# The order of a chunk's products in the recurrence of an RWKV-7 mixer: the keys' products ahead of the state's

## The chip, the core and the metric

The kernel runs on one core of one Trainium2 chip. The metric is the device time of one execution in microseconds, as the median of several runs. The profile is of one execution, and it shows each engine's instructions: TensorE (PE, with its weight loads as PEld), VectorE (DVE), ScalarE (ACT), GpSimd (POOL) and SyncE (SP), which issues the DMAs.

## What is computed

One decoder layer over 512 tokens of width 1024: a combined projection, a dilated attention, an RWKV-7 time mixing, gates, an output projection and a gated feed-forward part with a short convolution. The change lies in the time mixing, which for each of 16 heads (64 by 64 state) is this recurrence over the tokens:

```python
def step(state, inp):
    r_t, w_t, k_t, v_t, aa_t, bb_t = inp
    sa = jnp.einsum('bhvk,bhk->bhv', state, aa_t)
    state = state * w_t[:, :, None, :] + sa[..., None] * bb_t[:, :, None, :] + v_t[..., None] * k_t[:, :, None, :]
    return state, jnp.einsum('bhvk,bhk->bhv', state, r_t)
```

Each token's `sa` depends on the state, and so on the tokens before it.

## The kernel before

**Stages.** First come the attention's projections and scores, then, in one long stage written with a planner (`rwkv`, line 1041), the projections of the time mixing, the recurrence, the branch gates and the attention's output projection; then the mixer's output, and the feed-forward part with its up and down products. Float32 products of weights are made of three products of halves (high by high, high by low, low by high, lines 156 to 172), each with 512 moving columns.

**The recurrence.** It doesn't go token by token. 512 tokens are cut into 8 chunks of 64 (`NCH`, line 31). The 16 heads are 8 pairs, and a group g (0 to 3) holds two pairs, i = 0 and 1, four heads. `pair` (line 1223) prepares r, k, v and the scaled rows of a pair; its `ar` holds for each chunk the rows that are multiplied with the state, one half for what is solved for and one half for the outputs, and `gt` holds the masked products of these rows with the keys. `inverse` (line 1436) turns the triangular system of each chunk into a matrix, mostly on VectorE in many short steps (tiles `tt` and `lt`, lines 1500 to 1526). `chain` (line 1572) then goes through the 8 chunks c of a group, and these steps follow each other for each chunk:

- `values` and `value` (1591 to 1602): v of two chunks on TensorE into the PSUM tile `u`, then two copies on ScalarE into the tile `uv`. They are made once for two chunks, behind the update of an odd chunk, for the next two.
- `state` (1625): the right-hand side of what is solved for, in the PSUM tile `xy`: the state's share (two products, `ar` with the state `mbd`, 128 rows by 64 columns of the array, 128 moving columns; not for c = 0) and the keys' share (four products, `gt` with `uv`, 64 by 64, 64 moving columns).
- `state_out` (1633): the state's share of the outputs, two products like those of the state above, in the PSUM tile `xo`.
- `xs` (1639) copies `xy` on ScalarE, `solve` (1649) multiplies with the inverse, `solved` (1653) copies the result into `uv`.
- `update` (1656): four products for the new state into the other half of the tile `u`; `carry` (1661) makes the new state `mbd` of each pair from it on VectorE; `mp` (1643) has scaled the old one on GpSimd before.
- `outs` and `out` (1668 to 1675): the keys' share of the outputs, added in `xo`, and its copy.

**What sets the order.** `Plan` (line 47) holds tasks with an engine, an estimated time in microseconds, what they depend on, a priority (a smaller number goes first) and rooms in buffers that they take and give back. Its `run` (line 68) simulates the engines by these estimates, with 0.2 between engines, and emits each task's instructions when the simulation starts it. So it fixes the order on each engine; on the chip each engine works through that order and waits on semaphores. Tasks of the chain have priority 0 or a little over it (`C_`), the steps of evicting PSUM 1, weights 2 and more, the products of the projections 10 and more, the pairs' work and the inverse about 200. So a product of a projection goes where TensorE would have nothing of the chain to do: these are the fillers, and the rows of the timeline name their tiles (pg for the gates, pa for the attention's output, k, r and v for the projections of the pairs). A filler is booked at 0.237 (line 1119).

The lines that book the two tasks of the change, before it:

```python
st = pe(0.6 if c else 0.33, state, [uvd[c], start] + mb, take=("xy",), name=f"xy{g}.{c}")
so_ = pe(0.33 if c else 0.0, state_out, [st], C_ + 0.01, take=("xo",), name="xo")
x = sca(0.29, xs, [st], take=("xs",), give=("xy",))
```

`state` depends on the values (`uvd`) and on the carried state (`mb`) alike; in the plan it starts when both are there.

Of the kernel before, what the change touches and what calls it, by code (L numbers as in the profile page):

```python
# [18 lines left out]
P = 128  # L19
# [98 lines left out]
C_, E_, W_, V_, I_, M_, S_, U_ = 0.0, 1.0, 2.0, 200.0, 200.15, 220.0, 1.0, 10.0  # L118
# [10 lines left out]
class Layer:  # L129
# [1442 lines left out]
    def chain(self, g):  # L1572

        nc, pl, cw = self.nc, self.pl, self.cw
        prs, gr = self.prs[g], self.grp[g]
        ps = lambda s, **kw: self.cps.tile([P, 512], F32, tag=s, name=self.n(s), **kw)
        mbd = lambda i: self.mbd[2 * (g % 2) + i]
# [4 lines left out]
        pe = lambda us, fn, deps, prio=C_, **kw: pl.add("PE", us, fn, deps, prio, **kw)  # L1582
# [27 lines left out]
        def vals(c):  # L1610
            t = pe(0.54, lambda: values(c), [start, last_uv])
            t = sca(0.38, lambda: value(c, 0), [t], C_, take=("uv",))
            uvd[c] = uvd[c + 1] = sca(0.38, lambda: value(c, 1), [t], C_)
        vals(0)
        for c in range(NCH):
            e, q, cp = c % 2, c // 4, (c % 4) // 2

            R = [slice(64 * (e ^ i), 64 * (e ^ i) + 64) for i in range(2)]
            X = R[::-1]
            gt = lambda i, h, rows, cols, e=e, q=q, cp=cp: prs[i]["gt"][rows, e ^ i, 4 * q + 2 * cp + h, cols]  # L1620
            s = {}

            ih = [(i, h, slice(h * 64, h * 64 + 64), slice(i * P + h * 64, i * P + h * 64 + 64)) for h in range(2) for i in range(2)]

            def state(c=c, s=s, gt=gt, R=R, X=X, ih=ih):
                xy = s["xy"] = ps("xy")
                s["uv"] = uvs[c - c % 2][:, c % 2]
                for i in range(2 if c else 0):
                    self.mm(xy[X[i], :P], prs[i]["ar"][:, c, X[i]], mbd(i), True, False)
                for i, h, cs, ci in ih:  # L1630
                    self.mm(xy[X[i], cs], gt(i, h, R[i], X[i]), s["uv"][R[i], ci], c == 0 and h == 0, h == 1)

            def state_out(c=c, s=s, R=R):

                s["xo"] = ps("xo")
                for i in range(2 if c else 0):
                    self.mm(s["xo"][R[i], :P], prs[i]["ar"][:, c, R[i]], mbd(i), True, False)

            def xs(s=s):
                s["xs"] = cw.tile([P, P], F32, tag="xs", name=self.n("xs"), bufs=1)  # L1640
                nc.scalar.copy(s["xs"], s["xy"][:, :P])

            def mp(c=c, s=s):
                s["mp"] = cw.tile([P, 2, P], F32, tag="mp", name=self.n("mp"), bufs=1)
                for i in range(2):
                    nc.gpsimd.tensor_scalar(s["mp"][:, i, :], mbd(i), prs[i]["pc"][:, c : c + 1], 0.0, op0=ALU.mult,
                                            op1=ALU.add)

            def solve(s=s, gt=gt, X=X, ih=ih):
                for i, h, cs, _ in ih:  # L1650
                    self.mm(d["u"][X[i], cs], gt(i, h, X[i], X[i]), s["xs"][X[i], cs], h == 0, h == 1)

            def solved(i, s=s, X=X):
                nc.scalar.copy(s["uv"][X[i], i * P : i * P + P], d["u"][X[i], :P])

            def update(c=c, q=q, s=s):
                for j, (i, h, cs) in enumerate(hs):
                    self.mm(d["w"][64 * h : 64 * h + 64, cs], prs[i]["bkt"][q][:, c % 4, 64 * h : 64 * h + 64],
                            s["uv"][:, cs], j < 2, j > 1)

            def carry(i, c=c, s=s):
                ws, pc = d["w"][:, i * P : (i + 1) * P], prs[i]["pc"][:, c : c + 1]
                if c:
                    nc.vector.scalar_tensor_tensor(mbd(i), ws, pc, s["mp"][:, i, :], op0=ALU.mult, op1=ALU.add)
                else:
                    nc.vector.tensor_scalar(mbd(i), ws, pc, 0.0, op0=ALU.mult, op1=ALU.add)

            def outs(c=c, s=s, gt=gt, R=R, ih=ih):
                for i, h, cs, ci in ih:
                    self.mm(s["xo"][R[i], cs], gt(i, h, slice(0, P), R[i]), s["uv"][:, ci], c == 0 and h == 0, h == 1)  # L1670

            def out(c=c, s=s):
                if c % 2 == 0:
                    yts[c // 2] = cw.tile([P, 2, P], F32, tag=f"yt{c // 2}", name=self.n("yt"), bufs=1)
                nc.scalar.copy(yts[c // 2][:, c % 2, :], s["xo"][:, :P])

            st = pe(0.6 if c else 0.33, state, [uvd[c], start] + mb, take=("xy",), name=f"xy{g}.{c}")
            so_ = pe(0.33 if c else 0.0, state_out, [st], C_ + 0.01, take=("xo",), name="xo")
            x = sca(0.29, xs, [st], take=("xs",), give=("xy",))
            mpt = pl.add("POOL", 1.06, mp, mb, C_, take=("mp",)) if 0 < c < NCH - 1 else None  # L1680
            so = pe(0.33, solve, [x, last_uv], give=("xs",), name="u")
            last_uv = sca(0.28, lambda solved=solved: solved(0), [so])
            last_uv = sca(0.28, lambda solved=solved: solved(1), [last_uv])
            prev = mb
            if c < NCH - 1:
                up = pe(0.5, update, [last_uv], name="w")
                mb = [dve(0.36, lambda i=i, carry=carry: carry(i), [up, mpt, so_], give=("mp",) if mpt and i else ())
                      for i in range(2)]
            if e and c < NCH - 1:
                vals(c + 1)  # L1690
            ou = pe(0.35, outs, [last_uv, so_], C_ + 0.02, name="xr")
            yt = sca(0.29, out, [ou], C_ + 0.05, take=("yts",) if c == 0 else (), give=("xo",))
            used.extend([ou] + ([up] if c < NCH - 1 else []))
            if e:
                pl.join(used, give=("uv",))
                used = []
            d["yt", c] = yt
            if e:
                norms.append(self.norm(yts, c // 2, [yt, d["yt", c - 1]], T_))
# [474 lines left out]
```

## Time and profile before

| | us |
|---|---|
| median of 3 runs | 1232.48 |
| lowest, highest | 1231.15, 1234.05 |
| the profiled execution | 1231.16 |
| its span in the trace | 1229.4 |
| recurrence of g0, first to last xy product | 443.6 to about 488 |
| recurrence of g3, to its last xy product | from 708.5 to 750 |

The span is what the trace shows from the first to the last instruction; the rest of the execution's own time lies around it. The granted clock of TensorE is 0.982 of full speed over the span. In the page, busy times are given with their share of the span; a matmul's end is modelled, so that products which follow each other overlap in the rows, and the distance of two starts says what one costs. In a row of the timeline stand start, length, engine, line, operation, the tile written and the tiles read, the tile of the array (rows * columns) for a matmul, partitions by elements and type, and the count of records that were merged; in brackets the idle time of the engine before it and what ended it. Products of float32 are recorded as two passes each. All matmuls stand at line 148, the helper that issues them, so they are told apart by the tiles they write and read.

### The profile page before, as it was taken

Reading aid. Unit: us, or ns where it says so; the run is one execution under the profiler, and the core shown is the slowest. Engines: PE = TensorE matmul, PEld = TensorE weight load, DVE = VectorE, ACT = ScalarE, POOL = GpSimd, SP = SyncE. Lnnn points to the kernel's source line nnn. Section 1 sums busy time; section 2 is a strip of 40 time slices with the busy share of each in tenths; the row PEclk is TensorE's granted clock in tenths of the full one; section 3 lists DMA queues with packets and bytes.
Section 4 is the critical chain, followed back from the end, with each engine's and each line's share of the span. In section 5 each row is a group of like instructions: output and inputs, shape, how many; then the busy total and the mean of one; then the engine's idle time right before and its main releaser. Section 6 shows DMA issues by size and latency. Waiting matters only on the chain.

```text
span 1229.4 us, 18443 instructions
## 1 busy us (share of the span) xinstructions
PE 1179.8 (96%) x7188; PEld 946.3 (77%) x7188; DVE 746.0 (61%) x1254; ACT 542.6 (44%) x1009; POOL 120.3 (10%) x235
## 2 busy tenths in 40 slices
PE   4999999999999999999999599999999999999997
PEld 3788888889777876767776467788888888878886
DVE  6687862431678977846896844665556555652135
ACT  4384621522566364464544443444444444442123
POOL 4000000000001013131103122214000000000001
PEclk9899999999999999999999699999999999999999
DMA  9845871130233332413231525560232323333331
GB/s 317 248 142 157 284 236 46 52 86 5 81 100 84 98 108 72 127 44 116 78 99 49 159 60 177 154 206 18 69 103 86 103 86 103 86 103 103 103 120 69
DMA packets 168902, 139.41 MB, mean 113 GB/s; under 512 B 8849, under 2 KB 150251, under 8 KB 168815
## 3 DMA queue, kind: packets, MB, share of 16 engines
q1 hardware_dynamic: 168671, 137.98, 37.0%
q8 instruction: 56, 0.92, 0.3%
q14 instruction: 31, 0.25, 0.1%
q10 hardware_dynamic: 144, 0.26, 0.1%
HBM read 127.65 MB, written 10.56 MB: 112 GB/s over the span
## 4 chain that ended last, share of the span: by engine, by line
PE 82%; DVE 9%; DMA 4%; ACT 2%; issue 1%; SPq 0%; POOL 0%; POOLq 0%; DVEq 0%; ACTq 0%
PE u L148 22%; PE o L148 13%; PE v L148 7%; PE pg L148 7%; PE qk L148 6%; PE pr L148 3%; PE r L148 3%; PE k L148 3%; PE pa L148 3%; DMA araw<-in_w_ada_dram 2%; PE early L148 2%; PE po L148 2%; PE xy L148 2%; PE pt L151 1%; PE xo L148 1%
## 5 line engine op out<-in xcount | busy, mean ns | idle before, releaser
L194 DVE TENSOR_TENSOR wlo<-raw,whi 128x1024 fp32r<-128x1024 f32 x67 | 83.9, 1252 | 152.6 <-ACT whi L193 152.6
L148 PE MATMUL u<-h2lo,whi 128*128 128x512 f32 (+2 forms) x368 | 142.3, 387 | 0.0
L148 PE MATMUL u<-h2hi,whi 128*128 128x512 f32 (+2 forms) x368 | 142.2, 387 | 0.0
L148 PE MATMUL u<-h2hi,wlo 128*128 128x512 f32 (+2 forms) x368 | 142.2, 386 | 0.0
L1136 ACT CAST whi<-raw 128x1024 fp32r<-128x1024 f32 (+2 forms) x73 | 72.5, 994 | 122.7 <-PE qk L148 49.5
L193 ACT CAST whi<-raw 128x1024 fp32r<-128x1024 f32 x67 | 70.3, 1049 | 112.1 <-PE o L148 53.8
L1139 DVE TENSOR_TENSOR wlo<-raw,whi 128x1024 fp32r<-128x1024 f32 (+2 forms) x73 | 83.7, 1149 | 19.1 <-ACT whi L1136 18.8
L148 PEld LDWEIGHTS u<-h2lo,whi 128*128 128x128 f32 x368 | 68.9, 187 | 15.8 <-POOL h2lo L405 0.2
L148 PEld LDWEIGHTS u<-h2hi,wlo 128*128 128x128 f32 x368 | 68.9, 187 | 15.7
L148 PEld LDWEIGHTS u<-h2hi,whi 128*128 128x128 f32 x368 | 68.9, 187 | 15.4
L2019 DVE SCALAR_TENSOR_TENSOR u<-u,cols,u 128x511 f32<-128x511 f32 x88 | 65.7, 746 | 4.3 <-ACT u L2017 2.7
L148 PE MATMUL qk<-hhi,wlo 128*128 128x512 f32 x160 | 64.0, 400 | 0.0
L148 PE MATMUL qk<-hlo,whi 128*128 128x512 f32 x160 | 63.6, 397 | 0.0
L148 PE MATMUL qk<-hhi,whi 128*128 128x512 f32 x160 | 63.5, 397 | 0.0
L148 PE MATMUL o<-whi,fhi 128*128 128x512 f32 x144 | 56.1, 390 | 0.3 <-DVE u L2019 0.3
L148 PE MATMUL o<-whi,flo 128*128 128x512 f32 x144 | 56.0, 389 | 0.0
L148 PE MATMUL o<-wlo,fhi 128*128 128x512 f32 x144 | 56.0, 389 | 0.0
L148 PE MATMUL pg<-hhi,wlo 128*128 128x512 f32 x128 | 51.8, 405 | 0.0
L148 PE MATMUL pg<-hlo,whi 128*128 128x512 f32 x128 | 51.7, 404 | 0.0
L148 PE MATMUL pg<-hhi,whi 128*128 128x512 f32 x128 | 51.7, 404 | 0.0
L810 DVE CUSTOM_DVE_ANT_0 sm<-sc,m 128x256 f32<-128x256 f32 (+1 forms) x64 | 23.9, 404 | 37.6 <-PE sc L148 36.5
L347 DVE SCALAR_TENSOR_TENSOR acc<-araw,cols,acc 128x1024 f32<-128x1024 f32 x28 | 35.9, 1281 | 15.9 <-DMA araw<-in_w_ada_dram 15.8
(409 smaller groups left out, 2779.1 us busy)
## 6 DMA issues: line engine op xcount, KB each, us to landing
raw<-in_w_in_dram SPq DMA_DIRECT2D x62, 512.0 KB
raw<-in_w_up_dram SPq DMA_DIRECT2D x44, 512.0 KB
araw<-in_w_ada_dram SPq DMA_DIRECT2D x32, 512.0 KB
raw<-in_w_down_dram SPq DMA_DIRECT2D x22, 512.0 KB
araw<-in_w_ada_dram SPq DMA_DIRECT2D x32, 256.0 KB
wvraw<-in_w_in_dram SPq DMA_DIRECT2D x20, 256.0 KB
gate_d<-gs SPq DMA_DIRECT2D x16, 256.0 KB
gate<-gate_d SPq DMA_DIRECT2D x16, 256.0 KB
```

The source lines that it names most:

```text
L148: return self.nc.tensor.matmul(out, lhsT, rhs, start=start, stop=stop)
L151: self.nc.tensor.matmul(out, in_, self.ident[: in_.shape[0], : in_.shape[0]], is_transpose=True, start=start, stop=stop,)
L193: self.nc.scalar.copy(hl[0], raw)
L194: (lo_eng or self.nc.vector).tensor_tensor(hl[1], raw, hl[0], op=ALU.subtract)
L347: nc.vector.scalar_tensor_tensor(d["acc"], raw, ck, d["acc"], op0=ALU.mult, op1=ALU.add)
L810: nc.vector.tensor_tensor_reduce(d["sm", h][:, :wd], d["sc"][h][:, :wd], m[:, 256 - wd : 256] if gi == 0 else m[:, :wd], 1.0, 3.0e38, op0= ...
L1136: nc.scalar.copy(d["w"][0], d["raw"])
L1139: nc.vector.tensor_tensor(d["w"][1], d["raw"], d["w"][0], op=ALU.subtract)
L2019: nc.vector.scalar_tensor_tensor(u[:, d:], pu[:, : S - d], ch(c), u[:, d:], op0=ALU.mult, op1=ALU.add)
```

## The change

Within `state` the four products of the keys' share go first and open the accumulation in `xy`, and the two products of the state's share follow and close it. `state_out` is booked at 0.24 instead of 0.33, and its priority becomes -1 instead of 0.01, so that nothing else that is ready on TensorE goes between the two tasks. What is summed up is the same; only the order of the sums in `xy` differs.

```diff
             def state(c=c, s=s, gt=gt, R=R, X=X, ih=ih):
                 xy = s["xy"] = ps("xy")
                 s["uv"] = uvs[c - c % 2][:, c % 2]
+                for i, h, cs, ci in ih:
+                    self.mm(xy[X[i], cs], gt(i, h, R[i], X[i]), s["uv"][R[i], ci], h == 0, c == 0 and h == 1)
                 for i in range(2 if c else 0):
-                    self.mm(xy[X[i], :P], prs[i]["ar"][:, c, X[i]], mbd(i), True, False)
-                for i, h, cs, ci in ih:
-                    self.mm(xy[X[i], cs], gt(i, h, R[i], X[i]), s["uv"][R[i], ci], c == 0 and h == 0, h == 1)
+                    self.mm(xy[X[i], :P], prs[i]["ar"][:, c, X[i]], mbd(i), False, True)
...
             st = pe(0.6 if c else 0.33, state, [uvd[c], start] + mb, take=("xy",), name=f"xy{g}.{c}")
-            so_ = pe(0.33 if c else 0.0, state_out, [st], C_ + 0.01, take=("xo",), name="xo")
+            so_ = pe(0.24 if c else 0.0, state_out, [st], C_ - 1.0, take=("xo",), name="xo")
             x = sca(0.29, xs, [st], take=("xs",), give=("xy",))
```

## The prediction

> **What bounds the kernel now.** The page first, for the share of each engine and for the chain that ended last.
>
> ```profile
> span 1229.4 us, 18443 instructions
> PE 1179.8 (96%) x7188; PEld 946.3 (77%) x7188; DVE 746.0 (61%) x1254; ACT 542.6 (44%) x1009; POOL 120.3 (10%) x235
> PE 82%; DVE 9%; DMA 4%; ACT 2%; issue 1%; SPq 0%; POOL 0%; POOLq 0%; DVEq 0%; ACTq 0%
> ```
>
> TensorE is busy for 96% of the span and carries 82% of the last chain, so a microsecond taken from its queue can count in full. An average says nothing about one stage, so the busy times by window come next, cut at the recurrences of the four groups (g0 to g3). The columns are window, length, then PE, PEld, DVE, ACT and POOL busy time, granted clock, DMA share, GB/s.
>
> ```profile
> 440.00:490.00 50.00, 50.00 (x481) 34.96 (x480) 34.53 (x84) 27.15 (x70) 13.59 (x26) 1.00 0.29 84
> 515.00:560.00 45.00, 44.68 (x447) 30.73 (x447) 22.86 (x42) 25.79 (x66) 13.22 (x23) 1.00 0.27 77
> 640.00:690.00 50.00, 46.87 (x462) 32.18 (x460) 37.39 (x89) 23.19 (x64) 13.53 (x25) 0.94 0.26 82
> 690.00:706.00 16.00, 5.58 (x135) 4.68 (x137) 13.59 (x24) 8.67 (x15) 2.17 (x3) 0.50 0.59 166
> 706.00:755.00 49.00, 49.00 (x440) 32.63 (x439) 20.40 (x42) 21.09 (x61) 10.46 (x22) 0.94 0.25 74
> ```
>
> The recurrences of g0, g1 and g3 run with TensorE full (50.00 of 50, 44.68 of 45, 49.00 of 49): products of the projections fill what a chunk leaves free. Between g2 and g3 lies the one hole, 690 to 706: TensorE 5.58 of 16, VectorE 13.59 of 16. There VectorE decides. So there are two kinds of place: where TensorE is full, its own time for a chunk counts; in the hole, what lets VectorE finish the inverse of g3 sooner.
>
> **What the change saves on TensorE.** The timeline of TensorE over an odd chunk, c = 5 of g0, and the update after it. Here xy<-mbd is the state's share of what is solved for, xy<-uv the keys' share, xo<-mbd the state's share of the outputs; 4 or 8 records are the passes of 2 or 4 products.
>
> ```profile
> 474.11 0.40 PE L148 MATMUL pg<-hhi,wlo 128*128 128x512 f32 x1
> 474.44 0.44 PE L148 MATMUL xy<-mbd,ar 128*64 128x128 f32 x4
> 474.81 0.45 PE L148 MATMUL xy<-uv,gt 64*64 64x64 f32 x8
> 475.19 0.44 PE L148 MATMUL xo<-mbd,ar 128*64 128x128 f32 x4
> 475.56 0.50 PE L148 MATMUL pg<-hhi,whi 128*128 128x512 f32 x1
> ...
> 477.95 0.45 PE L148 MATMUL u<-uv,bkt 128*64 128x64 f32 x8
> 478.24 0.61 PE L148 MATMUL u<-cen,v 128*64 128x128 f32 x8
> 478.68 0.40 PE L148 MATMUL xo<-uv,gt 128*64 128x64 f32 x8
> ```
>
> Read the starts, since the ends are modelled. The three groups take 0.37, 0.38 and 0.37 us, and the array's tiling goes 128*128, 128*64, 64*64, 128*64, 128*128: four switches. The lower rows show the same kind of product between neighbours of its own tiling: u<-cen,v, eight records of 128x128 at 128*64, starts at 478.24 and is followed at 478.68, so eight take 0.44 and four take 0.22. Between two switches four take 0.37. The change puts the 64*64 group first, then both 128*64 groups behind each other: one switch fewer, and 0.37 - 0.22 = 0.15 us less.
>
> How often: the rows of the two groups, by tile.
>
> ```profile
> L148 PE MATMUL xy<-mbd,ar x112: 272/323/474, 449.1 to 749.5; 128*64 128x128 f32 x112
> L148 PE MATMUL xo<-mbd,ar x112: 272/323/473, 449.9 to 750.3; 128*64 128x128 f32 x112
> ```
>
> 112 records by 4 are 28 chunks: c = 1 to 7 of four groups (c = 0 has no state, and its products don't change). In the timeline of all 28 the xo group already stands right behind the xy group, so the new priority of the outputs' share moves nothing by itself. Saved at most: 28 x 0.15 = 4.2 us.
>
> **What it costs: the keys' values are the later arrival.** An even chunk, c = 6 of g0, in the timeline of all engines. VectorE's carry makes mbd, ScalarE's two copies (L1602) make uv.
>
> ```profile
> 478.96 0.61 DVE L1664 SCALAR_TENSOR_TENSOR mbd<-u,pc,mp 128x128 f32<-128x128 f32 x2 [1.78 <-PE u L148]
> ...
> 479.66 0.76 ACT L1602 COPY uv<-u 64x256 f32<-64x256 f32 x2 [2.41 <-DVE mbd L1664]
> ...
> 480.13 0.44 PE L148 MATMUL xy<-mbd,ar 128*64 128x128 f32 x4
> ...
> 480.50 0.45 PE L148 MATMUL xy<-uv,gt 64*64 64x64 f32 x8
> ```
>
> mbd is ready at 479.57 (478.96 + 0.61), uv at 480.42 (479.66 + 0.76), because both read the PSUM tile u and the copies wait for the carry. Today the state's products run from 480.13 to 480.50 and cover just this lateness. With the keys first nothing does: the queue stands from 480.13 until 480.42, about 0.30 with the start. The planner won't put the chunk later: it books the values as before. That TensorE waits for uv in just this way shows in c = 4 of g0, the first even chunk where uv is late; the last is c = 6 of g3.
>
> ```profile
> 468.37 0.53 PE L148 MATMUL xy<-mbd,ar 128*64 128x128 f32 x4
> 468.45 0.37 ACT L1602 COPY uv<-u 64x256 f32<-64x256 f32 x1 [0.49 <-DVE mbd L1664]
> ...
> 468.83 0.48 PE L148 MATMUL xy<-uv,gt 64*64 64x64 f32 x8
> ```
>
> ```profile
> 743.41 0.76 ACT L1602 COPY uv<-u 64x256 f32<-64x256 f32 x2 [2.43 <-DVE mbd L1664]
> ...
> 743.87 0.44 PE L148 MATMUL xy<-mbd,ar 128*64 128x128 f32 x4
> ```
>
> In the first, the copy ends at 468.82 and the keys start at 468.83; the new queue would stand from 468.37 to 468.83, 0.46. In the last, the copies end at 744.17 and the place in the queue is 743.87: 0.30. So it is in 9 of the 12 even chunks c = 2, 4, 6: two in g0, three in g1, one in g2, three in g3. Together 8 x 0.30 + 0.46 = 2.9 us of standing. Odd chunks take values copied a chunk earlier and don't wait.
>
> The Trainium skill (TensorE: Matmul & The Clock Gate, Part 2, on what happens when a matmul is issued) says that only weight loads are pulled ahead and that the matmuls stay in program order; this speaks against the change, and the row at 468.83 agrees. Were the products behind free to overtake a waiting one, nothing of the 2.9 would be lost.
>
> **Where the keys first do help.** Where mbd is the later arrival the keys fill the wait: c = 4 and c = 7 of g2.
>
> ```profile
> 667.27 0.92 PE L148 MATMUL xy<-mbd,ar 128*64 128x128 f32 x4
> ...
> 667.36 0.35 DVE L1664 SCALAR_TENSOR_TENSOR mbd<-u,pc,mp 128x128 f32<-128x128 f32 x1 [0.51 <-ACT uv L1602]
> ...
> 668.12 0.45 PE L148 MATMUL xy<-uv,gt 64*64 64x64 f32 x8
> ```
>
> ```profile
> 684.75 0.95 PE L148 MATMUL xy<-mbd,ar 128*64 128x128 f32 x4 [1.49 <-DVE mbd L1664]
> 685.63 0.69 PE L148 MATMUL xy<-uv,gt 64*64 64x64 f32 x8
> 686.25 0.69 PE L148 MATMUL xo<-mbd,ar 128*64 128x128 f32 x4
> ```
>
> At c = 4 the group takes 0.85 instead of 0.37 since the second carry is late; the keys (0.38) fit into that: 0.4 saved. At c = 7 the keys (0.62 at the lower clock) fit into the wait of 1.49; but the hole follows, so I count neither these 0.62 nor the 0.15 of that chunk.
>
> **The sum.** On TensorE: -27 x 0.15 + 2.9 - 0.4 = -1.55 us. By group: g0 -1.05 + 0.76 = -0.3; g1 -1.05 + 0.90 = -0.15; g2 (c = 1 to 6) -0.90 + 0.30 - 0.40 = -1.0; g3 -1.05 + 0.90 = -0.15. g3's share reaches the end, as only full TensorE follows at once. The rest has to pass the hole, which ends when VectorE is through.
>
> ```profile
> 659.98 0.61 DVE L1664 SCALAR_TENSOR_TENSOR mbd<-u,pc,mp 128x128 f32<-128x128 f32 x2 [2.87 <-PE u L148]
> ...
> 678.75 0.61 DVE L1664 SCALAR_TENSOR_TENSOR mbd<-u,pc,mp 128x128 f32<-128x128 f32 x2 [0.94 <-ACT uv L1602]
> 679.28 0.56 DVE L1512 TENSOR_TENSOR tt<-tt,lt 128x400 f32<-128x400 f32 x1
> ...
> 705.49 0.27 DVE L1589 MEMSET u<- 128x256 f32 x1
> ```
>
> VectorE works through its queue in order, and g3's inverse (tt, lt) stands behind the carries, which wait for the chunk: 2.87 us at 659.98, still 0.94 at 678.75. From there it hardly stands until the memset at 705.49 that starts g3. So what g2 saves up to its fifth chunk (-0.85) passes. Of g0 and g1 (-0.45) I count half: between them and g2 lies a stretch where VectorE is nearly full. That gives -0.15 - 0.85 - 0.2 = -1.2 us. Bounds of this case: -0.15 if only g3's share arrives, -1.55 if all does.
>
> **The planner's number.** 0.33 becomes 0.24, so the plan thinks each of 28 chunks 0.09 shorter, 2.5 us in all. Near the change it moves nothing: before the solve it still fits two filler products (0.6 + 0.24 + 2 x 0.237 = 1.31, against a copy ready at 0.6 + 0.2 + 0.29 + 0.2 = 1.29, by its own costs). Further off a step may change places; I take 0, and bound it by one to three such steps as the one of 0.56 at 679.28, either way: about 1.5 us.
>
> So the profiled execution (1231.16 us, span 1229.4) would become 1230.0. It lies 1.3 below the median of the runs, 1232.48; from that, -1.2 gives 1231.3 us. A measurement of this kernel can tell about 0.2%, 2.5 us, from no change: this is no measurable change.
>
> **Rivals.** *The values come in time.* If the plan's shift puts one more filler ahead of the even chunks, or ScalarE's copies go ahead of the carry, nothing stands: -27 x 0.15 - 0.4 = -4.45, 1228.0 us, faster. For it: in 3 of the 12 even chunks uv isn't late today. Against: 9 are late by nearly the same 0.30, and copies and carry follow each other. The Trainium skill (PSUM — Partial Sum Buffer, on bank collisions) holds that two engines must not touch one bank at once, reads included; the copy that starts at 479.66, 0.09 behind the carry's end, fits that, so only a change of their order would help.
>
> *The hole grows.* The plan thinks the chunks shorter while the even ones get 0.15 longer (0.30 - 0.15), so VectorE stands longer at g2's carries, with g3's inverse behind them. If at each of six carries one step of 0.56 goes from before the wait to behind it, the hole ends 6 x 0.56 = 3.4 us later: 1232.5 + 3.4 less g3's 0.15, 1235.7 us, slower. For it: the wait of 2.87 at 659.98 shows that such waits occur with nothing in front. Against: the carries at 678.75 and 684 hardly wait. It decides once the memset that starts g3 comes over 2.5 us later than at 705.49.
>
> *Joining saves nothing,* because the second pair of weights costs a start of its own: then 2.9 - 0.4 = +2.5 us is left, 1235.0, at the edge of slower. Against it stand the eight records in 0.44.
>
> **How the numbers follow.** Forecast 0.57, values in time 0.23, hole 0.15, no saving 0.05. Part of the forecast's case, with the 1.5 us of the plan in its favour, passes -2.5: I give that 0.03. Faster 0.23 + 0.03 = 0.26; slower 0.15 and half of the last, 0.17; same 0.57. The forecast's own range is 1231.3 with 1.5 of the plan and its bounds, 1229.4 to 1233.8. To leave out no more than 2 in 10 the range must reach both outer cases: 1228.0 to 1235.7.
>
> **What would show it.** Right: xy<-uv ahead of xy<-mbd and xo<-mbd in all 28 chunks; the two mbd groups together about 0.60 instead of 0.37 + 0.37; waits of PE xy for ACT uv L1602 of about 0.3 in most even chunks, nearly 3 us in sum; the memset of g3 about 1 us earlier; g3 from there to its last chunk unchanged within 0.3. Wrong: no such waits (the first rival), a hole that ends over 2.5 us later (the second), or 0.74 for the joined groups (the third).

## The result, and the profile after

The changed kernel takes 1242.82 us (median of 3 runs, 1242.26 to 1244.67) against 1232.48: ratio 1.0084, 95% interval 1.0062 to 1.0105. It is 10.3 us slower; the prediction had 1231.3 and a range up to 1235.7. The profiled execution took 1242.26 us. Its page:

```profile
span 1240.5 us, 18454 instructions
PE 1182.6 (95%) x7188; PEld 948.6 (76%) x7188; DVE 746.9 (60%) x1254; ACT 542.3 (44%) x1009; POOL 119.6 (10%) x235
PE 78%; DVE 12%; DMA 4%; ACT 2%; issue 2%; POOL 1%; SPq 0%; POOLq 0%; DVEq 0%; ACTq 0%
```

The counts of each engine's instructions are those of before. TensorE is busy 2.8 us longer, and of the 11.1 us of span the other 8.3 are time in which it is idle. VectorE's share of the last chain rises from 9% to 12%. So most of the loss is waiting, not work on TensorE, and the chain points to VectorE. The 2.8 us are taken up in the last section.

Where, is read by cutting both traces at the same four points, the memsets (L1589) that start g0 to g3. The windows before, and then after; the columns are window, length, then busy time with records of PE, PEld, DVE, ACT and POOL, granted clock, DMA share and GB/s:

```profile
441.16:513.32 72.16, 72.11 (x703) 52.66 (x702) 52.67 (x109) 35.76 (x84) 16.90 (x30) 1.00 0.34 99
513.32:641.88 128.56, 127.75 (x1004) 97.35 (x1003) 93.63 (x165) 69.51 (x134) 19.93 (x34) 1.00 0.30 85
641.88:705.49 63.61, 50.38 (x587) 35.14 (x585) 48.66 (x107) 29.80 (x75) 15.70 (x28) 0.83 0.35 104
705.49:880.00 174.51, 171.09 (x1020) 133.70 (x1021) 93.72 (x154) 74.92 (x156) 42.19 (x68) 0.98 0.37 114
```

```profile
441.31:515.42 74.11, 72.08 (x699) 53.62 (x698) 56.75 (x114) 38.76 (x87) 17.01 (x30) 0.98 0.33 95
515.42:646.74 131.32, 128.69 (x1007) 98.13 (x1006) 90.03 (x160) 66.22 (x130) 17.74 (x34) 1.00 0.30 84
646.74:720.66 73.92, 62.83 (x640) 44.80 (x640) 57.48 (x121) 34.88 (x83) 15.99 (x28) 0.91 0.36 110
720.66:880.00 159.34, 148.74 (x921) 115.20 (x920) 77.86 (x131) 64.67 (x141) 43.35 (x68) 0.98 0.36 112
```

The first stretch is 1.95 us longer, the second 2.76, and the third, which ends with the hole, 10.31: the memset of g3 comes 15.2 us later than before. Yet the span grows by only 11.1. The third stretch shows why: TensorE worked 62.83 us in it instead of 50.38, on 640 records instead of 587. What it did there in advance, filler products of the attention's output, needn't be done later, and from the memset of g3 to the end of the span it is 519.8 us instead of 523.9: 4.1 us are given back. What isn't given back shows as idle TensorE (length less busy). It grows from 0.05 to 2.0 us in the first stretch and from 0.8 to 2.6 in the second. In the third it even falls, from 13.2 to 11.1, and behind the memset it rises from 3.4 to 10.6: there TensorE waits 3.2 us for a gate and 2.0, 1.7 and 1.1 for tiles of g3's outputs (yhi, yt, y), where before it waited 1.7 for a gate and 1.3 for the mixer's output (mhi). The likely reason, which no run tests, is that the fillers which could have stood in these waits are done by then.

**In the hole.** VectorE's timeline before, the last three steps (L1504) of g3's inverse and the transpose behind them:

```profile
689.22 0.63 DVE L1504 TENSOR_TENSOR tt<-tt,lt 128x450 f32<-128x450 f32 x1
...
690.75 0.64 DVE L1504 TENSOR_TENSOR tt<-tt,lt 128x465 f32<-128x465 f32 x1
...
692.09 0.69 DVE L1504 TENSOR_TENSOR tt<-tt,lt 128x512 f32<-128x512 f32 x1
...
693.54 1.06 DVE L1521 STREAM_TRANSPOSE tt<-tt 128x512 f32<-128x512 f32 x1
```

And after:

```profile
697.34 0.62 DVE L1504 TENSOR_TENSOR tt<-tt,lt 128x450 f32<-128x450 f32 x1
697.99 0.62 DVE L1505 TENSOR_REDUCE tt<-tt 128x15 f32<-128x450 f32 x1
698.53 0.87 DVE L1765 SCALAR_TENSOR_TENSOR y<-t,cols,y 128x256 f32<-128x256 f32 x2
699.31 1.28 DVE L1139 TENSOR_TENSOR wlo<-raw,whi 128x512 fp32r<-128x512 f32 x2
...
702.66 1.41 DVE L1743 SCALAR_TENSOR_TENSOR y<-y,cols,gg 128x512 f32<-128x512 f32 x2
703.99 0.64 DVE L1504 TENSOR_TENSOR tt<-tt,lt 128x465 f32<-128x465 f32 x1
...
709.13 1.29 DVE L1139 TENSOR_TENSOR wlo<-raw,whi 128x512 fp32r<-128x512 f32 x2
710.34 0.68 DVE L1504 TENSOR_TENSOR tt<-tt,lt 128x512 f32<-128x512 f32 x1
...
711.78 1.09 DVE L1521 STREAM_TRANSPOSE tt<-tt 128x512 f32<-128x512 f32 x1
```

From the first of the three to the transpose it was 4.3 us; now it is 14.4. Between them stand steps of g2's outputs (y), halves of the groups' outputs (ylo), and steps of the attention's output (alo, gate) and of its weights (wlo). In the plan these have priorities from 1 to 150 and the inverse has 200.75: whenever both are ready, the inverse goes last. Before, its last steps were emitted just before that stage opened; after, the plan's small shift lets the stage open three steps too early. These 10.1 us aren't the whole of the stretch: counted from g2's memset the first of the three comes 3.3 us later than before (50.6 instead of 47.3), and from the transpose to g3's memset it is 3.1 shorter (8.9 instead of 12.0). VectorE is never idle between the rows shown for longer than 0.23 us; it only does other work first. The Trainium skill (TensorE: Matmul & The Clock Gate, Part 1, Architectural detail) calls VectorE's queue strictly first in, first out, and the rows agree: the input of the step at 703.99 was done at 698.61 (the sum behind the first step, 697.99 + 0.62), and yet it begins only where the steps that start at 702.66 end (1.41 later, within 0.1).

**At the start of g1** TensorE's timeline shows a second thing. Before:

```profile
508.34 0.39 PE L148 MATMUL k<-hhi,whi 128*128 128x512 f32 x1
508.66 1.20 PE L148 MATMUL pe<-lt,gt 32*32 32x32 f32 x64
...
511.26 1.20 PE L148 MATMUL pe<-tt,lt 32*32 32x32 f32 x64
```

And after:

```profile
506.81 0.39 PE L148 MATMUL pg<-hhi,wlo 128*128 128x512 f32 x1
508.31 1.20 PE L148 MATMUL pe<-lt,gt 32*32 32x32 f32 x64 [1.11 <-DVE lt L1526]
...
511.34 1.48 PE L148 MATMUL pe<-tt,lt 32*32 32x32 f32 x64 [0.86 <-DVE lt L1567]
```

Before, projection products filled TensorE up to both of these pe products, and it waited for neither; after, the order that the plan emitted has too few products in front of them, and it stands 1.11 + 0.86 us, which is the idle time that the first stretch has gained. The pe products themselves are not late for it. On VectorE, though, three steps of a pair's work (from 511.32) now stand ahead of the second copy (L1569 at 513.43, 512.58 before), and a weight's step (514.15, 1.22 long) ahead of the memset, so that g1 starts 2.1 us later.

**The chunk itself** came out as predicted. TensorE's timeline after, an odd chunk, and an even one with the copy of the keys' values that it needs:

```profile
449.32 0.45 PE L148 MATMUL xy<-uv,gt 64*64 64x64 f32 x8
449.70 0.44 PE L148 MATMUL xy<-mbd,ar 128*64 128x128 f32 x4
449.97 0.39 PE L148 MATMUL xo<-mbd,ar 128*64 128x128 f32 x4
450.29 0.44 PE L151 MATMUL pt<-ident,bk 128*128 128x128 f32 x2
```

```profile
476.84 0.76 ACT L1602 COPY uv<-u 64x256 f32<-64x256 f32 x2 [2.41 <-DVE tt L1512]
...
477.32 0.78 PE L148 MATMUL xy<-uv,gt 64*64 64x64 f32 x8
...
478.03 0.44 PE L148 MATMUL xy<-mbd,ar 128*64 128x128 f32 x4
```

By the starts: 0.38 + 0.27 + 0.32 = 0.97 in the odd chunk, where 1.12 stood before, 0.15 less. In the even one the keys' group takes 0.71 instead of 0.38 because it waits 0.33 for the copy.

### The profile page after: what moved, and what is told of

Read it like the earlier page. It is cut to its first block, busy times and chain, and to the rows that moved or that the text cites. A ratio compares the mean times of both kernels' runs of the same rounds, so it can differ in the third digit from the quotient of the medians.

```text
span 1240.5 us, 18454 instructions
## 1 busy us (share of the span) xinstructions
PE 1182.6 (95%) x7188; PEld 948.6 (76%) x7188; DVE 746.9 (60%) x1254; ACT 542.3 (44%) x1009; POOL 119.6 (10%) x235
## 4 chain that ended last, share of the span: by engine, by line
PE 78%; DVE 12%; DMA 4%; ACT 2%; issue 2%; POOL 1%; SPq 0%; POOLq 0%; DVEq 0%; ACTq 0%
PE u L148 22%; PE o L148 13%; PE v L148 7%; PE qk L148 7%; PE pg L148 6%; PE k L148 3%; PE r L148 2%; PE po L148 2%; PE pr L148 2%; PE xy L148 2%; DMA araw<-in_w_ada_dram 2%; PE pa L148 2%; PE pt L151 2%; PE early L148 1%; DVE tt L1514 1%
```

## The experiments

Two things are joined in the change: the order of the products, and the booking of the outputs' share (with its priority). The theory: the order does what was predicted, a little over 1 us; the 10 us are the planner's, since 0.24 instead of 0.33 makes it emit another order on every engine. The rivals are that the products' new order is itself the cost, and that the booking costs in proportion to its error. Medians of before in the same sessions were 1231.53 to 1232.61.

**The order alone,** booked as before.

```diff
-            so_ = pe(0.24 if c else 0.0, state_out, [st], C_ - 1.0, take=("xo",), name="xo")
+            so_ = pe(0.33 if c else 0.0, state_out, [st], C_ + 0.01, take=("xo",), name="xo")
```

(against the changed kernel). 

> The new order of the products alone; the booking stays 0.33 with priority 0.01, so that VectorE, ScalarE, GpSimd and the DMAs have the order of the kernel before, and on TensorE only the products within state change places. Theory P (the booking of 0.24 rearranges the whole plan, and that costs the 11 us): about the kernel before, from 1.6 us faster to 0.2 slower, as the prediction's sum for the products had it. Theory Q (waiting for the keys' values lengthens each even chunk, and the chain of the recurrence with VectorE's queue behind it costs the 11 us): 8 to 11 us slower.

Measured: 1230.74, ratio 0.9989 (0.9975 to 1.0003). The memset of g3 is at 704.52, 1.0 earlier than before. Leaving out c = 7 of g2, which runs into the hole, the 27 other blocks (the xy products and the state's share of xo, from their start to the next product's) take 29.5 us instead of 31.1: 1.6 saved, where 1.55 was predicted; nine even chunks wait, 0.29 to 0.46 each.

**The booking alone,** the products in the old order.

```diff
-            so_ = pe(0.33 if c else 0.0, state_out, [st], C_ + 0.01, take=("xo",), name="xo")
+            so_ = pe(0.24 if c else 0.0, state_out, [st], C_ - 1.0, take=("xo",), name="xo")
```

> The booking alone (0.24, priority -1); the products within state in the order before. Theory P: slower by 9 to 13 us, with the memset that starts g3 at about 720 instead of 705.5, as in the changed kernel. Theory Q: within 2 us of the kernel before.

Measured: 1245.39, ratio 1.0111 (1.0091 to 1.0131), memset of g3 at 722.87. The whole loss is here, without a single product moved within a chunk. (The priority does nothing by itself: with 0.33 and -1 the emitted program is that of before.)

**Other bookings,** keys first, priority as before.

```diff
+            so_ = pe(0.34 if c else 0.0, state_out, [st], C_ + 0.01, take=("xo",), name="xo")
```

> Keys first, as in the changed kernel, and the outputs' share booked at 0.34 instead of 0.24 (priority 0.01). Theory S (any booking gives another plan, and the plans scatter by several us, whichever way the number goes): somewhere between 3 us faster and 13 slower than the kernel before, not tied to the size of the step. Rival B (a booking that is too short is what harms, in proportion): as keys first with 0.33, 1.4 us faster, within 1.5.

> Keys first and a booking of 0.30. Theory S: not tied to the step; anything from 3 us faster to 13 slower. Rival B: a third of the way from 0.33 to 0.24, so about 3 us slower than the kernel before, between the two.

> Keys first in all chunks, the outputs' share booked at 0.20 (priority as before). Booked at 0.34 it measured -0.5 us, at 0.33 -1.4, at 0.30 +12, at 0.24 (the change) +11. Theory that the time is scattered over plans, with no rule in the booking: anywhere between -3 and +13 us, and where it is slow the memset of g3 is late by more than the end. Rival that the booking's error is what costs, more with each step: +13 us or more, and the memset of g3 later than the 723.7 of 0.30.

Measured, with 0.34: 1231.42, ratio 0.9996 (0.9980 to 1.0012). With 0.30: 1244.61, 1.0097 (1.0067 to 1.0128). With 0.20: 1236.37, 1.0040 (1.0024 to 1.0057). So a third of the change's step costs as much as all of it, and a larger one costs less: cost in proportion is refuted. The time is not tied to the size of the step; what each booking does to the order is seen only in its own trace.

**The last steps of the inverse ahead.** If the overtaking in the hole is the cause there, raising these three steps must undo it.

```diff
-            t = dve(0.37 + cost(1, j), lambda j=j: step(j), [t], name=f"inv{g}")
+            t = dve(0.37 + cost(1, j), lambda j=j: step(j), [t], 0.5 if g == 3 else I, name=f"inv{g}")
```

In the changed kernel: 

> The changed kernel, and of g3's inverse the last three steps (lines 1543 and 1544) with priority 0.5 instead of 200.75. The order of the instructions differs from the changed kernel's only from there to the end of the stage. Theory H (most is lost in the hole: from 695.7 on, VectorE does 12 us of the attention's output, weights and evictions between and ahead of these three steps, and the recurrence of g3 starts late): the memset that starts g3 goes from 14 us behind the before's to 5 to 8 behind it, and 4 to 8 of the 11 us come back. Rival E (it is lost earlier, at the starts of g1 and g2, which come 2.1 and 4.8 us later, or behind the hole): less than 2 us come back.

In the kernel before: 

> The control: the same priority in the kernel before. Theory H: the last steps were through there before the attention's output began, so within 1.5 us of the kernel before. If raising the priority is a gain by itself, whatever the plan: 3 us faster or more.

In the kernel with 0.30: 

> Keys first, booked at 0.30 as in the run that measured 1.0097, and the last three steps of g3's inverse at priority 0.5. In that run the steps' starts lie at 700.45, 710.66 and 713.69 with work of the attention's output between them, and the memset of g3 at 723.7. Theory that the overtaking of these steps is what the plans share: the memset comes at 713 to 717 and 3 to 6 us come back, ratio 1.005 to 1.008. Rival that the overtaking belongs to the one plan of the change, and the loss of 0.30 has another place: 1.009 or more.

Measured: 1239.21, ratio 1.0056 (1.0036 to 1.0077), in the changed kernel; 1229.14, 0.9970 (0.9955 to 0.9985), in the one before; 1243.72, 1.0094 (1.0068 to 1.0120), with 0.30. In the changed kernel the three steps follow each other again in VectorE's timeline:

```profile
696.15 1.00 DVE L1504 TENSOR_TENSOR tt<-tt,lt 128x450 f32<-128x450 f32 x1
...
697.85 0.64 DVE L1504 TENSOR_TENSOR tt<-tt,lt 128x465 f32<-128x465 f32 x1
...
699.20 0.69 DVE L1504 TENSOR_TENSOR tt<-tt,lt 128x512 f32<-128x512 f32 x1
...
711.36 0.27 DVE L1589 MEMSET u<- 128x256 f32 x1
```

The memset comes 9.3 us earlier than in the changed kernel and 5.9 behind the one before, as expected, but the median falls by only 3.6, a little less than the 4 to 8 that I expected; the two intervals, 1.0062 to 1.0105 without the edit and 1.0036 to 1.0077 with it, overlap. The windows of this kernel, and then of the one with 0.30, without and with the edit, show why:

```profile
647.06:711.36 64.30, 48.34 (x586) 34.08 (x585) 48.21 (x105) 29.83 (x75) 15.51 (x28) 0.86 0.31 98
711.36:880.00 168.64, 164.11 (x992) 129.38 (x993) 89.54 (x150) 71.94 (x153) 41.02 (x68) 0.98 0.37 117
```

```profile
650.34:723.72 73.38, 58.20 (x623) 41.72 (x622) 56.12 (x119) 34.03 (x82) 16.27 (x28) 0.91 0.34 102
723.72:880.00 156.28, 150.09 (x918) 115.12 (x917) 77.44 (x131) 64.05 (x140) 43.53 (x68) 0.98 0.35 114
```

```profile
645.84:710.69 64.85, 47.00 (x583) 33.85 (x581) 48.31 (x105) 29.74 (x75) 15.75 (x28) 0.86 0.30 93
710.69:880.00 169.31, 165.27 (x985) 129.78 (x986) 89.25 (x149) 70.93 (x151) 41.08 (x68) 0.96 0.38 117
```

With 0.30 the stretch from g2 to g3 falls by 8.5 us with the edit, so its plan had the same overtaking; but TensorE then does 583 records in it instead of 623, its idle time there rises from 15.2 to 17.9, and from the memset to the end it takes 527.2 us instead of 520.3. Of 8.5 us, 6.9 go back. The 3 to 6 us that I expected there did not come: the ratios agree within their intervals. (The profiled execution with the edit, 1239.64 us, is the lowest of its four, and g0's memset lies 4.6 us earlier in it, ahead of all that the edit touches.) A shorter hole is worth only what fillers had not used it for. In the kernel before I had expected no gain beyond 1.5 us, and 3.5 came (1229.14 against 1232.61): a y step stood ahead of the last transpose there too, and from the first transpose to g3's memset, 12.0 us before (693.54 to 705.49), it is now 8.6 (692.96 to 701.56).

The control bears on the changed kernel too. The raised priority is worth 3.5 us where only one y step had gone ahead of the last transpose, so the 3.6 us of the changed kernel do not show what the overtaking cost. With the edit in both kernels the change still costs 10.1 us (1239.21 against 1229.14, one session), against 10.3 without it. By the stretches of the profiled executions (the table below) it costs 1.9 and 2.8 us in the first two, as without the edit, and 4.2 less 0.6 in the last two, where without it there were 10.3 less 4.1: 2.6 us less, which the medians don't confirm. So the overtaking is shown to move g3's memset; that it makes the time is not shown.

**Which group's booking.** Still open was whether the late starts of g1 and g2 open the long hole, or whether each stretch is disturbed by itself.

```diff
+            so_ = pe((0.24 if g > 1 else 0.33) if c else 0.0, state_out, [st], C_ + 0.01, take=("xo",), name="xo")
```

> Keys first in all chunks, the outputs' share booked at 0.24 in g2 and g3 and at 0.33 in g0 and g1, so that the plan is that of the run with 0.33 (ratio 0.9989) up to g2's first chunks. If the booking disturbs each stretch by itself: the starts of g1 and g2 as there (513.1 and 641.4), the hole up to 10 us longer, +4 to +7 us, ratio 1.003 to 1.006. If the delays of g0 and g1 are what opens the hole: memset of g3 within 2 us of 704.5, ratio 0.998 to 1.001.

> Keys first in all chunks, booked at 0.24 in g0 and g1 and at 0.33 in g2 and g3, so that the plan is the change's up to the end of g1's chunks. If the booking disturbs each stretch by itself: g1 and g2 start 2 and 5 us late, and the hole is as long as before (62 to 66 us from g2's start to g3's): +4 to +5 us, ratio 1.002 to 1.005. If the early delays open the hole: 70 us or more from g2's start to g3's, ratio 1.006 to 1.010.

Measured: late (g2, g3) 1240.79, ratio 1.0081 (1.0064 to 1.0098); early (g0, g1) 1237.59, 1.0049 (1.0034 to 1.0064). The stretches of the late one, from g1 on, and then of the early one:

```profile
515.04:643.32 128.28, 127.56 (x1004) 98.06 (x1003) 93.68 (x166) 69.76 (x134) 19.93 (x34) 1.00 0.30 85
643.32:716.63 73.31, 61.54 (x640) 44.02 (x640) 57.25 (x120) 34.94 (x83) 15.54 (x28) 0.93 0.37 111
```

```profile
442.38:516.42 74.04, 71.96 (x700) 53.56 (x699) 56.79 (x114) 38.96 (x87) 17.02 (x30) 0.98 0.32 94
516.42:647.86 131.44, 128.80 (x1006) 98.12 (x1006) 90.08 (x160) 66.32 (x130) 17.80 (x34) 1.00 0.29 84
647.86:710.98 63.12, 47.79 (x587) 34.28 (x585) 48.51 (x107) 30.28 (x76) 15.52 (x28) 0.87 0.34 105
```

Late: 128.28 as before, and the hole's stretch 73.31. Early: the first two stretches of the change, and the hole's stretch 63.12, as short as before. So each disturbance belongs to the plan of its own groups. By the medians they don't add: 1.0081 and 1.0049 apart, 1.0084 together, and the late one cost more than the 1.003 to 1.006 that I gave it. In the profiled executions, from g0's memset to the end and against the order alone, they do: 6.6 and 4.7 us apart, 11.9 together. Both of these executions are the lowest of their four, so what the medians have more is in no trace, and stays open.

**Other orders at before's plan.** The state's two shares first and joined, keys last:

```diff
-                for i, h, cs, ci in ih:
+                for i, h, cs, ci in (() if c else ih):
...
+                for i, h, cs, ci in (ih if c else ()): self.mm(xy[X[i], cs], gt(i, h, R[i], X[i]), s["uv"][R[i], ci], False, h == 1)
```

(the second line stands in `state_out`, behind the outputs' share). 

> The booking and the plan of the kernel before; within a chunk the state's two shares go first, joined, and the keys' products last, so that one switch of tiling is saved and nothing waits for the keys' values (xy ends 0.22 us later). Theory P, with the prediction's price of 0.15 per joined pair: 1.0 to 4.2 us faster, blocks of 0.97 instead of 1.12 in all chunks where they waited for nothing. Theory Q: the chain of a chunk gets 0.22 longer, 28 x 0.22 = 6 us, so slower by 2 us or more.

Measured: 1232.36, ratio 0.9998 (0.9985 to 1.0011). Timeline of all engines, an even chunk of g0:

```profile
469.61 0.51 PE L148 MATMUL xy<-mbd,ar 128*64 128x128 f32 x4
469.67 0.37 ACT L1602 COPY uv<-u 64x256 f32<-64x256 f32 x1 [0.49 <-DVE mbd L1664]
470.06 0.27 ACT L1675 COPY yt<-xo 128x128 f32<-128x128 f32 x1
...
470.38 0.44 PE L148 MATMUL xo<-mbd,ar 128*64 128x128 f32 x4 [0.26 <-ACT yt L1675]
...
470.74 0.45 PE L148 MATMUL xy<-uv,gt 64*64 64x64 f32 x8
```

In the even chunks the join is lost again: the one buffer xo is still to be copied for the previous chunk, and ScalarE does that behind the values. Ten of their twelve blocks take 1.36 to 1.51 us, where 1.12 was usual, while the odd ones take 0.97; the 27 blocks together save 0.7 us. A new wait took the place of the old one, and neither theory came true: the time is that of before, neither 1 us faster nor 2 slower.

Keys first in odd chunks only, where they never wait:

```diff
+                for part in (mine if c % 2 else mine[::-1]):
+                    part()
```

(`mine` holds the keys' and the state's products). 

> The booking and the plan of the kernel before; keys first only in odd chunks, where the values were copied a chunk earlier; even chunks as before. Theory P: 16 x 0.15 = 2.4 us less on TensorE and no waits for the values, 0.6 to 2.4 us faster, so 1 to 2 us better than keys first everywhere. Theory Q: as the kernel before, within 1 us.

Measured: 1230.11, ratio 0.9987 (0.9976 to 0.9998). The 27 blocks take 28.9 us instead of 31.1, 2.3 less, as Theory P has it. By the medians that is 1.8 us faster than before and 0.6 faster than keys first everywhere; the intervals of the two orders overlap, so that one is better than the other is not shown.

**Both gains together,** this order and the inverse's last steps ahead, with before's booking. 

> The kernel before with two edits together: in odd chunks alone the keys' products go first (bookings as before), and the last three steps of g3's inverse have priority 0.5. Alone they measured 0.9987 and 0.9970, that is -1.6 and -3.7 us. If they save in different places (TensorE's queue in the full stretches, VectorE's order in the hole) they add: about -5 us, ratio 0.995 to 0.997, the memset of g3 at 699 to 701. Rival: the hole absorbs what the chunks of g0 to g2 save, so that the two together are no better than the priority alone: 0.997 to 0.998, memset at 701 or later.

Measured: 1227.80, ratio 0.9960 (0.9944 to 0.9976): faster than either kernel of the case, 4.1 us below the one before by the medians. From g0's memset (443.38) to g3's (702.60) it takes 259.2 us, against 264.3 before (705.49 - 441.16); the memset lies later than I wrote only because g0 began 2.2 later in this execution. From g0's memset to g3's the two alone take 262.4 and 260.8 us, so 1.9 and 3.5 saved apart and 5.1 together. The ratios say the same, 0.13% and 0.30% apart and 0.40% together, but the interval holds 0.9970 as well: that the gains add fits best, and the rival is not excluded by the time.

The stretches side by side (us; starts of the memsets, and the span's end):

| kernel | g0 to g1 | g1 to g2 | g2 to g3 | g3 to end | ratio |
|---|---|---|---|---|---|
| before | 72.2 | 128.6 | 63.6 | 523.9 | 1 |
| the change | 74.1 | 131.3 | 73.9 | 519.8 | 1.0084 |
| order alone | 71.8 | 128.3 | 63.1 | 524.0 | 0.9989 |
| booking alone | 74.5 | 132.3 | 74.5 | 520.6 | 1.0111 |
| booked 0.20 | 71.7 | 127.9 | 70.1 | 521.7 | 1.0040 |
| booked 0.24, g2 and g3 | 71.8 | 128.3 | 73.3 | 520.4 | 1.0081 |
| booked 0.24, g0 and g1 | 74.0 | 131.4 | 63.1 | 523.4 | 1.0049 |
| the change, inverse ahead | 74.1 | 131.4 | 64.3 | 525.0 | 1.0056 |
| before, inverse ahead | 72.2 | 128.6 | 60.1 | 525.6 | 0.9970 |
| booked 0.30 | 76.6 | 127.4 | 73.4 | 520.3 | 1.0097 |
| booked 0.30, inverse ahead | 76.6 | 127.5 | 64.9 | 527.2 | 1.0094 |
| keys first in odd chunks | 71.5 | 128.0 | 62.9 | 523.5 | 0.9987 |
| both gains | 71.6 | 128.0 | 59.6 | 524.0 | 0.9960 |

A row is read across: a long third column is partly repaid in the fourth; in the change and in its early half, a long first and second are not.

## Why the prediction was wrong

**The step that failed** is the planner's number: "Near the change it moves nothing", "I take 0, and bound it by one to three such steps". The booking alone is worth 13.5 us by medians of the same session (1245.39 against 1231.92). I checked the two fillers ahead of the solve in one chunk. But the plan adds up 28 chunks, and with them shifts the moment at which the attention's output opens, all of whose work goes ahead of the inverse. A bound made of the length of steps was of the wrong kind: a shift decides which of two tasks goes first, and 10.1 us of other work (14.4 - 4.3) went between three steps. The two halves of the booking show where it costs: in g0 and g1 through the stretches up to g2's memset (ratio 1.0049), in g2 and g3 through the stretch that ends with the hole (1.0081).

**The sum of the products** was right. -1.2 us was predicted for what arrives at the end, and the order alone gave -1.2 by medians of one session (1230.74 against 1231.92; the interval just includes no change). That they agree to a tenth is luck, since the interval reaches 1.7 us to either side; the blocks are the better evidence, 1.6 us saved against 1.55. The joined pair took 0.27 + 0.32 where 0.60 was forecast; the waits were about 0.3 in nine even chunks of the order alone, as forecast (0.29 to 0.46); in the change ten wait, 0.31 to 0.77 each. The Trainium skill (TensorEngine Tiling (Array Packing), Key Properties) has it that a change of the tiling mode drains TensorE. The rows agree in that a change costs time, and they give the price that the page doesn't: one change fewer, 0.15 us.

**The second rival** came nearest: "It decides once the memset that starts g3 comes over 2.5 us later", and it came 15.2 later. Its mechanism was not the right one. It moved single steps of the inverse behind the carries, priced at 3.4 us; the runs show other work going ahead of the inverse's last steps. With the steps put ahead the memset came 9.3 us earlier, so this part of the delay is shown; that it costs the time is not, since the same edit gains as much in the kernel before. The first rival (values in time) and the third (joining saves nothing) are refuted by the odd and even chunks.

**What passes the hole.** I had only asked what is late, not what the wait is filled with. The hole's stretch grew by 10.3 us, and 4.1 were repaid behind it.

**What stays open.** That the late starts of g1 and g2 (4.7 us together) come with the plan is shown by the early booking. Which of the swapped steps make them is read from the timeline at g1 alone (steps ahead of the second copy and of the memset on VectorE, fillers missing at the pe products); no run changed that one place. Nor is it shown which steps make the time that the late booking loses, as raising the last three of the inverse leaves the change as dear as it was, nor why the two halves cost more by their medians than their traces show.

## What to carry to other kernels

Where a planner emits the order, an estimated duration is part of the program: time a new order with the old bookings first and the booking by itself, and before forecasting either, look at which tasks change places near the next bottleneck, not only near the edit; the planner's own simulation can be asked for that before anything runs. The last steps of a serial chain that the critical engine is waiting for should have the priority of what they release; in the kernel before that was worth 3.5 us, more than the new order of the products (1.2), with 0.30 nothing that could be measured. An edit that is to mend something needs the control without the thing to mend: here the control gained as much, and the mending was not shown. And a stretch that grows is not lost time until one has counted what the critical engine did in it: compare its idle time to the end, not the date of a mark.

## What the runs showed of the hardware

The price of a change of tiling falls on both neighbours: four records of 128*64 took 0.37 us between two other tilings, 0.27 when the next group had the same tiling (449.70 to 449.97), and 0.32 when the one before had it (449.97 to 450.29). With the pair first and the keys behind, an odd chunk took the same 0.97.

A product of 512 columns that follows another without a wait started 0.23 us behind it where the granted clock was 1.00 (as in g0, 440 to 490 before), and 0.43 behind it where it was 0.50. In the changed kernel it was 0.50 from 512.70 to 515.20, as TensorE came back from its waits at the start of g1:

```profile
513.34 0.63 PE L148 MATMUL r<-hlo,whi 128*128 128x512 f32 x1
513.76 0.63 PE L148 MATMUL r<-hhi,wlo 128*128 128x512 f32 x1
```

Of such pairs 0.43 apart there are 43 in the change and 23 before: 20 x 0.2 = 4.0 us. Less the 1.1 that the 27 blocks save in the change (30.0 us instead of 31.1), this is close to the 2.8 us by which TensorE is busy longer. So fillers that the change moves into stretches of low clock cost nearly twice their time there.
